# Down products of three SwiGLU half-steps as seven products of quarters

## The chip, the cores and the metric

One core of one Trainium2 chip runs the whole program. The metric is device time in microseconds (us) of one execution; the kernel before was timed three times. TensorE is called PE here, VectorE DVE, ScalarE ACT, GpSimd POOL and SyncE, which issues the loads, SP.

## The reference

A trunk of two layers over 512 tokens of width 1024, in float32. Each layer is three steps, each ending in a LayerNorm: a SwiGLU half-step, token mixing, and another SwiGLU half-step. There are four half-steps in all, with weights of their own; `D_FF` is 2816.

```python
def swiglu(x, w_gate, w_up, w_down):
    return (jax.nn.silu(x @ w_gate) * (x @ w_up)) @ w_down
...
    for l in range(DEPTH):
        x = layer_norm(DEEPNORM_ALPHA * x + 0.5 * swiglu(x, ffn_w_gate[l, 0], ffn_w_up[l, 0],
                                                         ffn_w_down[l, 0]),
                       ln_g[l, 0], ln_b[l, 0])
...
        x = layer_norm(DEEPNORM_ALPHA * x + mix, ln_g[l, 1], ln_b[l, 1])
        x = layer_norm(DEEPNORM_ALPHA * x + 0.5 * swiglu(x, ffn_w_gate[l, 1], ffn_w_up[l, 1],
                                                         ffn_w_down[l, 1]),
                       ln_g[l, 2], ln_b[l, 2])
```

## The kernel before

Every float32 product is made of three passes in a rounded format (`mm3`, line 120): each operand is split into a high part and the rest, and high x high, high x rest and rest x high are summed in one PSUM bank. The split of an operand (`split`, line 88) takes one ACT instruction for the high part (line 90) and one DVE instruction for the rest (line 92). Weights come by 512 KB loads on SP's queue (`fetch`, line 102) into four buffers `raw`, and are split (`halves`, line 107) into five pairs of buffers `whi` and `wlo`. A load can go out as soon as its buffer is free, ahead of its use.

The four half-steps are calls of `ffn` (line 214): the first ends near 385 us of the profiled span, the mixing of layer 0 fills 385 to 610 us, half-steps 2 and 3 end near 985 and 1350, the mixing of layer 1 near 1475, and half-step 4 ends the program. A half-step has two parts:

- Up products: 11 groups `fg` of 256 columns of the gate and the up weights. A group takes four loads and 96 `mm3` passes' matmuls of 512 tokens into four of the eight PSUM banks. Then ACT makes a tanh (line 251) and DVE the gated product `th` (lines 252 and 254), which is split into `act[f]` (128 rows of h transposed, 512 tokens). All 22 chunks of `act` are kept.
- Down products: all eight banks hold the result, four token tiles by two halves of 512 columns. For each of the 22 chunks `F` one load of 128 full rows of the down weights serves 4 x 2 x 3 matmuls (`down`, line 260). The last four chunks are kept loaded and the token tiles are finished one after another; after each, `ln_tile` (line 151) adds the two banks to `alpha*x` on DVE (line 158), lets ACT sum squares (line 164), DVE scale (lines 167 and 176) and POOL work out the factor (lines 168, 140 and 141). The transposes of the new x back into `xh` and `xl` (`to_xt`, line 126) wait in a list, and `flush` puts them between later products; the last two tiles' transposes fall into the next part's first products, which start with the first 256 tokens for that reason. `load_next` (line 113) asks for the next part's first weights.

The order of the work on an engine comes from a scheduler, which places an instruction when what it waits for is ready and takes the one written earlier where several are. Only inside `as_written` (line 73) is the order of an engine that of the program; half-step 1 uses that for PE, the others do not. POOL issues no DMAs. In half-step 1 the parameters of the state-space mixer are prepared beside the products (`s5_prepare`, called at group 1), with DMAs of their own. Layer 0's mixing spills x to DRAM, and half-step 2 loads it back (`x_back`, line 1150) in the place where the program has it, between up and down products.

## Time and profile before

| | us |
|---|---|
| median of three runs | 1847.7 (1847.27 to 1848.16) |
| the profiled execution, its span | 1845.7 |
| PE busy | 1818.3 |
| DVE busy | 898.4 |
| ACT busy | 637.0 |
| POOL busy | 32.2 |

The span runs from the first to the last instruction of one execution. Matmuls are pipelined, so PE counts as busy while any matmul is in it. L12 in a row is line 12 of the kernel; `<-` stands between what an instruction writes and what it reads, and, in brackets or after the idle time, ahead of what ended a wait. A line can be that of a helper: all splits have lines 90 and 92.

### The profile page before, as it was taken

The page shows a single profiled execution, that of the slowest core. Times are in us where ns is not written, and L with a number is a line of the kernel's source. Part 1 is how long each engine was busy: PE and PEld are TensorE (multiplying, and loading weights), DVE is VectorE, ACT ScalarE, POOL GpSimd, SP SyncE. Part 2 cuts the span into 40 slices and gives each one's busy share as a digit, 9 for nine tenths or more (in the row PEclk, how much of TensorE's full clock was granted, in tenths as well). Part 3 has the DMA queues.
Part 4 walks back from the last instruction along what each step waited for, and adds up shares of the span by engine and source line. Part 5 has one row for each costly group of instructions (what it writes and reads, how often), then busy time and mean ns, then how long its engine had stood idle before and what let it go on. Part 6 is the DMA issues. An engine that isn't in the chain of part 4 may idle for free.

```text
span 1845.7 us, 22332 instructions
## 1 busy us (share of the span) xinstructions
PE 1818.3 (99%) x8896; PEld 1523.2 (83%) x8896; DVE 898.4 (49%) x1531; ACT 637.0 (35%) x971; POOL 32.2 (2%) x119
## 2 busy tenths in 40 slices
PE   8999999999999999999999999999999999999998
PEld 7888888888877888888889888888878898888886
DVE  7856542267766644433227334432388554343324
ACT  3233421246675432222115223221264332222211
POOL 0000000000000000000000000000010000000000
PEclk9999999999999999999999999999999999999999
DMA  6345623264412633332323333323333153333231
GB/s 206 105 125 166 205 96 103 91 193 132 153 55 92 205 115 100 95 102 93 98 97 104 102 94 100 97 98 93 118 101 104 47 149 92 103 92 103 92 103 57
DMA packets 158968, 206.48 MB, mean 112 GB/s; under 512 B 7696, under 2 KB 129808, under 8 KB 158864
## 3 DMA queue, kind: packets, MB, share of 16 engines
q1 hardware_dynamic: 158864, 205.06, 36.3%
q8 instruction: 69, 1.13, 0.3%
q14 instruction: 35, 0.29, 0.0%
HBM read 189.83 MB, written 14.16 MB: 111 GB/s over the span
## 4 chain that ended last, share of the span: by engine, by line
PE 72%; issue 22%; DVE 3%; ACT 1%; DMA 1%; POOL 1%; POOLq 0%; SPq 0%; DVEq 0%; ACTq 0%
PE ps L122 23%; PE ps L123 23%; PE ps L124 23%; PE ps L131 1%; PE ps L650 1%; DVE wlo L92 1%; DMA s5tl<-side 1%; PE ps L698 0%; POOL rs L141 0%; PE ps L690 0%; DMA x<-in_x_dram 0%; DVE pl L92 0%; ACT ps L164 0%; PE ps L689 0%; ACT whi L90 0%
## 5 line engine op out<-in xcount | busy, mean ns | idle before, releaser
L92 DVE TENSOR_TENSOR wlo<-raw,whi 128x1024 fp32r<-128x1024 f32 x313 | 382.6, 1222 | 593.0 <-ACT whi L90 592.0
L122 PE MATMUL ps<-xh,whi 128*128 128x512 f32 (+1 forms) x1696 | 635.9, 376 | 0.7 <-ACT xh L90 0.7
L123 PE MATMUL ps<-xl,whi 128*128 128x512 f32 (+1 forms) x1696 | 633.4, 374 | 2.8 <-DVE xl L92 2.8
L124 PE MATMUL ps<-xh,wlo 128*128 128x512 f32 (+1 forms) x1696 | 633.2, 374 | 0.0
L90 ACT ACTIVATE whi<-raw 128x1024 fp32r<-128x1024 f32 x313 | 330.7, 1058 | 823.0 <-PE ps L123 470.3
L122 PEld LDWEIGHTS ps<-xh,whi 128*128 128x128 f32 x1696 | 319.2, 189 | 59.8 <-issue 3.1
L123 PEld LDWEIGHTS ps<-xl,whi 128*128 128x128 f32 x1696 | 320.3, 189 | 58.0 <-DVE xl L92 3.3
L124 PEld LDWEIGHTS ps<-xh,wlo 128*128 128x128 f32 x1696 | 320.2, 189 | 56.7
L122 PE MATMUL ps<-whi,act 128*128 128x512 f32 x656 | 255.5, 390 | 0.0
L124 PE MATMUL ps<-whi,act 128*128 128x512 f32 x656 | 255.2, 389 | 0.0
L123 PE MATMUL ps<-wlo,act 128*128 128x512 f32 x656 | 255.2, 389 | 0.0
L124 PEld LDWEIGHTS ps<-whi,act 128*128 128x128 f32 x656 | 123.2, 188 | 25.5
L123 PEld LDWEIGHTS ps<-wlo,act 128*128 128x128 f32 x656 | 123.2, 188 | 25.4
L122 PEld LDWEIGHTS ps<-whi,act 128*128 128x128 f32 x656 | 123.2, 188 | 25.4
L252 DVE SCALAR_TENSOR_TENSOR th<-th,ps 128x512 f32<-128x512 f32 x88 | 59.8, 683 | 113.4 <-ACT th L251 113.4
L251 ACT ACTIVATE th<-ps 128x512 f32<-128x512 f32 x88 | 51.9, 595 | 155.1 <-PE ps L124 155.1
L254 DVE TENSOR_TENSOR th<-th,ps 128x512 f32<-128x512 f32 x88 | 59.7, 686 | 92.8 <-PE ps L124 92.8
L92 DVE TENSOR_TENSOR act<-th,act 128x512 fp32r<-128x512 f32 x82 | 52.7, 684 | 0.0
L122 PE MATMUL ps<-whi,xh 128*128 128x256 f32 (+1 forms) x160 | 49.6, 312 | 2.0 <-ACT whi L90 1.5
L123 PE MATMUL ps<-wlo,xh 128*128 128x256 f32 (+1 forms) x160 | 49.1, 307 | 2.2 <-DVE wlo L92 2.2
L90 ACT ACTIVATE act<-th 128x512 fp32r<-128x512 f32 x82 | 47.2, 617 | 7.6 <-DVE th L254 7.5
L124 PE MATMUL ps<-whi,xl 128*128 128x256 f32 (+1 forms) x160 | 48.5, 304 | 0.0
(303 smaller groups left out, 1360.2 us busy)
## 6 DMA issues: line engine op xcount, KB each, us to landing
raw<-in_wg_dram SPq DMA_DIRECT2D x88, 512.0 KB, 3.8
raw<-in_wu_dram SPq DMA_DIRECT2D x88, 512.0 KB, 3.8
raw<-in_wd_dram SPq DMA_DIRECT2D x88, 512.0 KB, 3.2
raw<-in_ab_in_dram SPq DMA_DIRECT2D x20, 512.0 KB, 4.5
raw<-in_cd_in_dram SPq DMA_DIRECT2D x12, 512.0 KB, 3.7
x<-in_x_dram SPq DMA_DIRECT2D x8, 512.0 KB, 6.7
s<-zf SPq DMA_DIRECT2D x8, 512.0 KB, 5.2
raw<-in_ab_out_dram SPq DMA_DIRECT2D x8, 512.0 KB, 4.2
```

The costliest lines, as they stand in the source:

```text
L90: nc.scalar.activation(out=hi, in_=src, func=AF.Copy, scale=scale)
L92: nc.vector.tensor_tensor(out=lo, in0=src, in1=hi.bitcast(F32), op=ALU.subtract)
L122: mm(ps, ah, bh, start=start, stop=False)
L123: mm(ps, ah, bl, start=False, stop=False)
L124: mm(ps, al, bh, start=False, stop=stop)
L131: self.nc.tensor.transpose(p[:, j * P:(j + 1) * P], src[:, k * P:(k + 1) * P], self.ident)
L251: nc.scalar.activation(out=th, in_=bk[0, f], func=AF.Tanh, scale=0.5)
L252: nc.vector.scalar_tensor_tensor(out=th, in0=th, scalar=1.0, in1=bk[0, f], op0=ALU.add, op1=ALU.mult)
L254: nc.vector.tensor_tensor(out=th, in0=th, in1=bk[1, f], op=ALU.mult)
L650: nc.tensor.matmul(banks[h][:, o:o + w], a[r, i * P:i * P + P], b[r, :w], start=n == 0, stop=n == 2)
```

## The change

Half-steps 2 to 4 call a new function `ffn7`. It sees the down product as a product of matrices of 2 x 2 blocks: h in two halves of 256 tokens and in even and odd chunks, the down weights in even and odd chunks (b1, b2) and two halves of 512 columns. Seven products of quarters take the place of eight. Of the seven weights three are quarters of the given ones and four are sums of quarters, `T1` to `T4`, kept in DRAM: `down_sums` copies quarters there and adds others onto them with DMAs that add, all issued from POOL. It is a generator in four steps, taken at every third group of up products one half-step ahead (`ahead`). The seven sums of h are made by DVE in `hb` after each group (four operations of 256 columns more than before) and split at once into a slot `sl` of 7 x 256 columns.

The 11 pairs of chunks are taken in three groups of 3, 4 and 4. A group's seven products run after the up product that follows the group's last (the last group's right after the last up product), so up and down products alternate. Each product is made for two token tiles of 128 in two banks; three of the seven (`P6`, `N3`, `P7`) go on top of what a bank holds already, after DVE has added it to x. `ln_tile` is cut into its addition (`add_to`) and the rest (`ln_rest`). `take` adds a finished pair of banks to the right quarter of x, with the sign. In the last group the LayerNorms of the first two token tiles are placed ahead of the last two products, and those of the other two behind each half of the last. PE's order is that of the program in `ffn7`. Half-step 1 and the mixers are unchanged. Comments and docstrings are removed.

```diff
-    def mm3(self, ps, ah, al, bh, bl, start, stop):
-        mm = self.nc.tensor.matmul
+    def mm3(self, ps, ah, al, bh, bl, start, stop, onto=False):
+        mm = partial(self.nc.tensor.matmul, skip_group_check=onto)
...
+    def add_to(self, zz, p, scale, total=None):
+        self.nc.vector.scalar_tensor_tensor(out=zz, in0=p, scalar=scale, in1=zz, op0=ALU.mult, op1=ALU.add,
+                                            **({} if total is None else {"accum_out": total}))
...
+                    if fg % 3 == 1:
+                        next(ahead, None)
...
+    def down_sums(self, wd):
+        dma = self.nc.gpsimd.dma_start
+        wv = wd.rearrange("(j two p) d -> two p j d", two=2, p=P)
+        b11, b12, b21, b22 = (wv[i][:, :, c:c + 512] for i in range(2) for c in (0, 512))
+        T = [self.dram.tile([P, NF // 2, 512], F32, name=f"T{i}_{len(self.sums)}") for i in range(1, 5)]
+        self.sums.append(T)
+        t1, t2, t3, t4 = T
+        for t, src in ((t3, b22), (t1, b12), (t2, b11), (t4, b21)):
+            dma(t, src)
+        yield
+        dma(t3, b12, accum_op=ALU.add)
+        dma(t1, b11, accum_op=ALU.add)
+        yield
+        dma(t2, t3, accum_op=ALU.add, max_dma_last_dim=2048)
+        yield
+        dma(t4, t2, accum_op=ALU.add, max_dma_last_dim=2048)
+    def ffn7(self, xt, wg, wu, wd, g_ap, b_ap, T, out=None, fetch=None, ahead=iter(()), groups=(3, 4, 4)):
+        nc, tc = self.nc, self.tc
+        tt = nc.vector.tensor_tensor
+        wv = wd.rearrange("(j two p) d -> two p j d", two=2, p=P)
+        t1, t2, t3, t4 = T
+        prod = {"P1": (0, wv[0][:, :, 0:512]), "P2": (1, wv[1][:, :, 0:512]), "Q5": (3, t1), "P6": (4, t2),
+                "N3": (6, wv[1][:, :, 512:]), "P7": (5, t3), "Q4": (2, t4)}
+        first = [sum(groups[:i]) for i in range(len(groups) + 1)]
+        with tc.tile_pool(name="act", bufs=1, reuse_waits="tile") as ap, \
+                tc.tile_pool(name="at", bufs=2, reuse_waits="tile") as at:
+            slots = {}
+            def up(fg):
+                bk, jobs = {}, []
+                for m, W in enumerate((wg, wu)):
+                    Wv = W.rearrange("(k p) f -> p k f", p=P)
+                    for f in range(2):
+                        bk[m, f] = self.bank()
+                    wt = [self.load(Wv[:, kh * 4:kh * 4 + 4, fg * 256:fg * 256 + 256], [4, 256]) for kh in range(2)]
+                    jobs.append(([(bk[m, f], f) for f in range(2)],
+                                 lambda k, f, wt=wt: [w[:, k % 4, f * P:f * P + P] for w in wt[k // 4]]))
+                    if not self.pending:
+                        self.cols(*jobs.pop())
+                if jobs:
+                    for m in range(2):
+                        self.cols(*jobs[m], 0, 256)
+                        self.flush(1 - m)
+                    for m in range(2):
+                        self.cols(*jobs[m], 256, SEQ)
+                hb = at.tile([P, 8, 256], F32, name="hb")
+                for f in range(2):
+                    th = at.tile([P, SEQ], F32, name="th")
+                    nc.scalar.activation(out=th, in_=bk[0, f], func=AF.Tanh, scale=0.5)
+                    nc.vector.scalar_tensor_tensor(out=th, in0=th, scalar=1.0, in1=bk[0, f],
+                                                   op0=ALU.add, op1=ALU.mult)
+                    tt(out=hb[:, 0::7] if f == 0 else hb[:, 1:3], in0=th.rearrange("p (a c) -> p a c", a=2),
+                       in1=bk[1, f].rearrange("p (a c) -> p a c", a=2), op=ALU.mult)
+                tt(out=hb[:, 3], in0=hb[:, 7], in1=hb[:, 2], op=ALU.subtract)
+                tt(out=hb[:, 5], in0=hb[:, 0], in1=hb[:, 7], op=ALU.subtract)
+                tt(out=hb[:, 4], in0=hb[:, 3], in1=hb[:, 0], op=ALU.subtract)
+                tt(out=hb[:, 6], in0=hb[:, 1], in1=hb[:, 4], op=ALU.add)
+                sl = ap.tile([P, 2, 7, 256], F32R, tag="sl", name="sl", bufs=max(groups) + 1)
+                self.split(hb[:, 0:7], sl[:, 0], sl[:, 1])
+                slots[fg] = sl
+            def fetch_w(name, js):
+                src = prod[name][1][:, js[0]:js[-1] + 1]
+                return self.load(src, [len(js), 512])
+            def part(name, banks, js, start, stop, w=None, ts=(0, 1)):
+                hi, lo = w or fetch_w(name, js)
+                b = prod[name][0]
+                for i, j in enumerate(js):
+                    for t in ts:
+                        c = slice(t * P, t * P + P)
+                        self.mm3(banks[t], slots[j][:, 0, b, c], slots[j][:, 1, b, c], hi[:, i], lo[:, i],
+                                 start and i == 0, stop and i == len(js) - 1, name in ("P6", "P7", "N3"))
+            def down(gi, ln):
+                last = gi == len(groups) - 1
+                js = list(range(first[gi], first[gi + 1]))
+                units = [js[i:i + 2] for i in range(0, len(js), 2)]
+                two = lambda: [self.bank() for _ in range(2)]
+                s = [self.sm.tile([P, 6], F32, name="st") for _ in range(NT)] if last else None
+                def take(banks, half, col, scale, total=None):
+                    for t in range(2):
+                        i = 2 * half + t
+                        self.add_to(xt[i][:, col * 512:col * 512 + 512], banks[t], scale,
+                                    s[i][:, total:total + 1] if last and total is not None else None)
+                def whole(name, banks, start=True):
+                    for u in units:
+                        part(name, banks, u, start and u is units[0], u is units[-1])
+                X, Y = two(), two()
+                if last:
+                    V = two()
+                    names = (("P1", X), ("P2", Y), ("Q5", V))
+                    for u in units:
+                        for name, bk in names:
+                            part(name, bk, u, u is units[0], u is units[-1])
+                    take(X, 0, 0, 0.25)
+                    take(Y, 0, 0, 0.25, 0)
+                else:
+                    whole("P1", X)
+                    take(X, 0, 0, 0.25)
+                    whole("P2", Y)
+                    take(Y, 0, 0, 0.25)
+                    V = two()
+                    whole("Q5", V)
+                take(V, 1, 1, 0.25)
+                whole("P6", X, False)
+                take(X, 0, 1, -0.25)
+                whole("N3", V, False)
+                take(V, 0, 1, 0.25, 1)
+                if last:
+                    g, b = self.ln_params(g_ap, b_ap)
+                def norm(t, junk):
+                    self.ln_rest(t, xt[t], s[t], junk, g, b, None if out is None else out[t * P:(t + 1) * P])
+                if last:
+                    norm(0, [V[0]] * 2)
+                    norm(1, [V[1]] * 2)
+                whole("P7", X, False)
+                take(X, 1, 1, -0.25, 1)
+                take(X, 1, 0, 0.25)
+                Z = two()
+                if not last:
+                    whole("Q4", Z)
+                    take(Z, 1, 0, 0.25)
+                    return
+                ws = [fetch_w("Q4", u) for u in units]
+                for t in range(2):
+                    for u, w in zip(units, ws):
+                        part("Q4", Z, u, u is units[0], u is units[-1], w, (t,))
+                    self.flush(1)
+                    self.load_next()
+                    self.add_to(xt[2 + t][:, 0:512], Z[t], 0.25, s[2 + t][:, 0:1])
+                    norm(2 + t, [Z[t]] * 2)
+            with self.as_written(mybir.EngineType.PE):
+                gi = 0
+                for fg in range(NF // 2):
+                    up(fg)
+                    if fg == 0 and fetch is not None:
+                        xt = fetch()
+                    if fg % 3 == 0:
+                        next(ahead, None)
+                    if gi < len(groups) - 1 and fg == first[gi + 1]:
+                        down(gi, False)
+                        gi += 1
+                down(gi, True)
...
-        k.ffn(None, wg[0, 0], wu[0, 0], wd[0, 0], ln_g[0, 0], ln_b[0, 0], spill=s0, side=side, fetch=x_again)
+        k.ffn(None, wg[0, 0], wu[0, 0], wd[0, 0], ln_g[0, 0], ln_b[0, 0], spill=s0, side=side, fetch=x_again,
+              ahead=k.down_sums(wd[0, 1]))
...
-        k.ffn(xt, wg[0, 1], wu[0, 1], wd[0, 1], ln_g[0, 2], ln_b[0, 2], fetch=x_back)
+        k.ffn7(xt, wg[0, 1], wu[0, 1], wd[0, 1], ln_g[0, 2], ln_b[0, 2], k.sums[0], fetch=x_back,
+               ahead=k.down_sums(wd[1, 0]))
         first(cd_in, 1024, 512)
-        k.ffn(xt, wg[1, 0], wu[1, 0], wd[1, 0], ln_g[1, 0], ln_b[1, 0])
+        k.ffn7(xt, wg[1, 0], wu[1, 0], wd[1, 0], ln_g[1, 0], ln_b[1, 0], k.sums[1],
+               ahead=k.down_sums(wd[1, 1]))
         first(wg[1, 1], 0, 256)
         k.mix_cd(cd_in, cd_out, pool_w, pool_s, sgu_ln, wsT, b_s, xt, ln_g[1, 1], ln_b[1, 1])
-        k.ffn(xt, wg[1, 1], wu[1, 1], wd[1, 1], ln_g[1, 2], ln_b[1, 2], out=out)
+        k.ffn7(xt, wg[1, 1], wu[1, 1], wd[1, 1], ln_g[1, 2], ln_b[1, 2], k.sums[2], out=out)
```

## Rows read from the trace of the kernel before

**Rows 1.** The page: busy time by engine, TensorE's clock in 40 slices.

```profile
PE 1818.3 (99%) x8896; PEld 1523.2 (83%) x8896; DVE 898.4 (49%) x1531; ACT 637.0 (35%) x971; POOL 32.2 (2%) x119
...
PEclk9999999999999999999999999999999999999999
```

**Rows 2.** What PE waited for, longest first: us in total, times, longest.

```profile
PE ps L131 <- DMA x<-in_x_dram: 6.1, 2, 4.4
```

**Rows 3.** Windows: up, then down products of half-step 2; busy us by engine.

```profile
core 0: us, PE busy (x) PEld busy (x) DVE busy (x) ACT busy (x) POOL busy (x), PEclk, DMA share, GB/s
700.00:760.00 60.00, 60.00 (x267) 49.69 (x266) 25.04 (x29) 17.72 (x23) 0.00 (x0) 1.00 0.34 99
900.00:950.00 50.00, 50.00 (x223) 41.40 (x222) 11.03 (x9) 9.55 (x9) 0.00 (x0) 1.00 0.29 100
```

**Rows 4.** Timeline of PE, down products: start, us, instruction; twelve apart.

```profile
880.12 0.39 PE L122 MATMUL ps<-whi,act 128*128 128x512 f32 x1
...
882.84 0.39 PE L122 MATMUL ps<-whi,act 128*128 128x512 f32 x1
```

**Rows 5.** Chain that ended last, half-step 2's end: start, us, what.

```profile
981.82 0.87 PE ps L131 x8
...
985.21 0.23 PE ps L124
985.67 0.12 PE ps L124
...
991.18 0.87 PE ps L131 x8
```

**Rows 6.** What the load queue (SP) waited for: us in total, times, longest.

```profile
SPq L104 <- DVE wlo L92: 1243.0, 267, 22.3
```

**Rows 7.** By line and shape, 620 to 980 us (last: whole): busy, mean ns.

```profile
L92 DVE TENSOR_TENSOR wlo<-raw,whi 128x1024 fp32r<-128x1024 f32 x65 | 79.7, 1226 | 150.3 <-ACT whi L90 150.1
L254 DVE TENSOR_TENSOR th<-th,ps 128x512 f32<-128x512 f32 x22 | 15.0, 687 | 27.0 <-PE ps L124 27.0
L92 DVE TENSOR_TENSOR act<-th,act 128x512 fp32r<-128x512 f32 x22 | 14.1, 684 | 0.0
L158 DVE SCALAR_TENSOR_TENSOR xb<-ps,xb 128x512 f32<-128x512 f32 x6 | 4.1, 692 | 3.8 <-PE ps L124 3.7
...
L90 ACT ACTIVATE whi<-raw 128x1024 fp32r<-128x1024 f32 x65 | 68.9, 1060 | 199.6 <-PE ps L123 116.6 <-PE ps L124 78.0 <-issue 2.8
L90 ACT ACTIVATE act<-th 128x512 fp32r<-128x512 f32 x22 | 12.5, 615 | 0.0
...
L485 DVE TENSOR_TENSOR xs<-xs 128x256 f32<-128x256 f32 x1 | 0.4, 426 | 0.0
```

**Rows 8.** Timeline of DVE: LayerNorm of tile 0 at half-step 2's end.

```profile
967.37 0.69 DVE L158 SCALAR_TENSOR_TENSOR xb<-ps,xb 128x512 f32<-128x512 f32 x1 [2.02 <-PE ps L124]
...
971.15 1.28 DVE L176 SCALAR_TENSOR_TENSOR zf<-zf,rs,lnb 128x1024 f32<-128x1024 f32 x1 [0.37 <-POOL rs L141]
```

**Rows 9.** Timeline of DVE: LayerNorm of the last tile.

```profile
1837.47 0.69 DVE L158 SCALAR_TENSOR_TENSOR xb<-ps,xb 128x512 f32<-128x512 f32 x1 [0.24 <-PE ps L124]
...
1841.25 1.41 DVE L173 SCALAR_TENSOR_TENSOR zf<-zf,rs,lnb 128x512 f32<-128x512 f32 x2 [1.51 <-POOL rs L141]
```

**Rows 10.** Timeline of POOL; loads of x back: count, ns, first and last issue.

```profile
0.99 0.46 POOL L491 MEMSET side<- 16x448 f32 x1
...
369.27 0.19 POOL L168 TENSOR_TENSOR st<-st 128x1 f32<-128x1 f32 x1 [358.68 <-ACT ps L164]
...
L1150 SPq DMA_DIRECT2D xb<-s x4: 320/362/478, 619.9 to 641.9; - x4
```

**Rows 11.** Windows: half-step 1.

```profile
0.00:369.00 369.00, 360.58 (x1700) 301.59 (x1701) 200.77 (x497) 113.28 (x143) 1.51 (x13) 1.00 0.44 137
```

**Rows 12.** Chain that ended last: first transposes ending half-steps 2 and 3.

```profile
975.49 0.88 PE ps L131 x8
...
1339.86 0.87 PE ps L131 x8
```

14 lines of the change are left out of this document (8 added, 6 removed).

## The prediction

> **What bounds the kernel now.** I read the page's totals first. TensorE (PE) is busy for 1818.3 of 1845.7 us and its clock was granted at the full level in every slice; VectorE (DVE) is busy for half the span and ScalarE (ACT) for a third [rows 1]. Next the waits: of all that PE waited for, the largest entry is 6.1 us in two waits for the first tiles of x [rows 2]. So no other engine holds PE back now, and a matmul that is taken away shortens the span by its whole spacing, unless the change makes a new wait. The stages confirm it: in 60 us of up products and in 50 us of down products of half-step 2, PE is busy throughout, DVE for 25.0 and 11.0 us, and the DMA engines for 0.34 and 0.29 of the time at about 100 GB/s [rows 3]. The reader should keep two things from there: PE has no gap to fill, and DVE has room on average, which says nothing of short stretches.
>
> **Matmuls removed.** The spacing of the down products is the distance of two starts, 882.84 - 880.12 = 2.72 us for 12 matmuls, 0.2267 us each [rows 4]. A half-step's down products are now 22 chunks x 4 token tiles x 2 halves x 3 passes = 528 matmuls. The change makes seven products of 11 chunks x 2 token tiles x 3 passes = 462, of the same shape (128 stationary columns, 512 moving). That is 66 x 0.2267 = 15.0 us for each of three half-steps: **-44.9 us**. Up products, transposes and LayerNorm counts stay. The order of PE is now pinned to the program's; around the end of half-step 2 it already went as the program has it (down products, transposes of the second tile at 981.82, last matmul at 985.21, then narrow up products from 985.67, the third tile's transposes at 991.18) [rows 5], so I cost the pin at nothing; where the scheduler's freedom had hidden a late operand, the price is that operand's lateness, 0 to 3 us for a half-step, which I count in the DVE terms below.
>
> **Weights in the down products.** Seven quarters instead of four are loaded and split: 7 x 11 = 77 half-width chunks against 44. A load of two chunks (512 KB) now serves 12 matmuls, 2.72 us, where one of the same size served 24. Supply: 0.524 MB / 2.72 us = 193 GB/s. Down loads (4 KB pieces) ran at 100 GB/s with 0.29 of the engines, 345 GB/s if they were full; up loads (1 KB pieces) at 99/0.34 = 291 [rows 3]. The 2 KB pieces lie between, so the down products need 0.56 to 0.66 of the engines while they run. At present the loads wait for a free buffer, not for the bus: the load queue spent 1243 us in 267 waits on DVE's releases [rows 6]. With nothing else on the bus I cost this at nothing; with something else, see the second rival.
>
> **DVE in a group of down products.** Prices [rows 7]: split of two chunks 1.226 us, of one 0.684; adding a bank to x 0.692; each multiplication of h 0.687; a 128x256 operation between SBUF tiles 0.426. The new split of seven quarters (1792 columns) has no row; along the line through 512 and 1024 columns, 1.06 ns a column, it is 2.04 us. For the group of three chunks: 7 x (1.226 + 0.684) = 13.4 us of splits, 16 additions of 0.69 = 11.0, the h work left after the up product (2 x 0.687 + 4 x 0.426 + 2.04) = 5.1, the first two splits for the next up product 2.5; less 3.1 for the splits made ahead (five buffers, two in use) and 1.4 for two additions that may come after: 27.5 us. PE takes 7 x 18 x 0.2267 = 28.6. That is 96% of DVE; a late split makes PE wait. Bounds 0 and 5 us, I take 1. The groups of four have 30.7 (17.2 + 11.0 + 5.1 + 2.5 - 3.7 - 1.4) against 38.1 us and are covered. The h work of the last up product is not one product ahead as in the other groups: 3.1 us on DVE, the ACT split (1.7 us on the line through its 512 and 1024 columns [rows 7]), 2.04 on DVE, about 7 us in all; ahead of its first use stand 42 matmuls, 9.5 us. Covered by 2.5 us, no cost. Additions to x stand one product (4.1 or 5.4 us) ahead of the next use of their bank and take 1.4 to 2.8 us: no cost either.
>
> **The end of a half-step.** The last group also has the LayerNorms. From the last matmul of product N3 to the transposes of tile 0 stand P7 (24) and a first half of Q4 (12 matmuls), 8.2 us. The chain of a tile took from the addition at 967.37 to the end of its last operation at 971.15 + 1.28, 5.1 us [rows 8]. So 3.1 us are spare, and DVE has about 12 us of work in the stretch (two LayerNorms, six additions, two splits), not all of it due there. Bounds 0 and 4 us a half-step, I take 2. Tiles 2 and 3 now follow each other at 2.7 us, not 5.4; in the next half-step's first up product they are due later than that, so no cost. At the kernel's end it counts: the last addition starts at 1837.47 and the final operations at 1841.25 [rows 9]; tile 2's last 1.41 us may now lie in tile 3's way. Bounds -0.7 (one addition less behind tile 3) and 1.4, I take 1.
>
> **The sums in DRAM.** Each set is four copies and four additions, each of 128 x 11 x 512 x 4 B = 2.88 MB, issued from POOL; three sets are 24 transfers. They have no PE, DVE or ACT work. The trace shows no DRAM-to-DRAM transfer and none from POOL. One transfer of that size takes the 16 engines 8.4 us at the rate of the down loads, 9.9 us at that of the up loads [rows 3]; an addition reads its target as well, so 8.4 to 19.8. Sum 202 to 356 us of all engines. Where they run matters: the code puts steps at every third group of up products, but what waits for nothing is moved forward. The loads of x back from DRAM, written behind all eleven up products of half-step 2, were issued at 619.9 to 641.9, and POOL's fill of line 491, which belongs to the second group, at 0.99 us [rows 10]. So I expect the twelve copies of all three sets near the kernel's start. There they share the bus with the first loads of x, for which PE waited twice [rows 2]: half the bus doubles a few us. Bounds 0 and 8, I take 3.
>
> **Sum.** -44.9 + 3 x 1 + 3 x 2 + 1 + 3 = -31.9 on the profiled span of 1845.7 us: 1813.8. The median of the runs is 2.0 us above the span, so **1816**. With all terms at their ends the case reaches from 1802 to 1839; 1802 to 1826 is its own range.
>
> **Rival 1, slower: POOL's queue.** POOL works out the factor of each LayerNorm in three small steps, the first of them at 369.27 [rows 10]. If all 24 transfers stand ahead of it, with each addition waiting in POOL's queue for what it adds to, then the LayerNorm of half-step 1 waits for nearly all of the 202 to 356 us, and PE with it, for the transposes and mixer need x. Until 369 us the kernel's own loads leave 56% of the engines, 207 us [rows 11]. Nothing is lost if the transfers need less. At 320 us, 93 us are lost (320 - 207, less some 20 for the last, which need only be issued): about 1910. It is slower than before from about 259 us on, 10.8 us a transfer (207 + 20 + the 32 us gained); at 356 us 1945, more if DRAM to DRAM is slower than any load shown. For it: the early issue of what waits for nothing [rows 10]; even the sums for half-step 4 wait for nothing but their own copies. Against it: sets 2 and 3 may be placed behind the LayerNorm, and at the rate of the down loads all is over in time.
> The Trainium skill, DMA: Bandwidth & Descriptors, "Anatomy of one DMA — SWDGE (gpsimd) path", says that DMA engines never wait on a semaphore: the wait is held by the issuing sequencer before it dispatches. This speaks against the change; by that rule the additions' waits stand in front of POOL's arithmetic and the time would be this rival's 1910, where transfers that hold up nothing leave it at 1816. The load queue's waits agree with it [rows 6]; no run here shows it for POOL.
>
> **Rival 2, DVE or the bus binds in the down products.** If splits come late in all nine groups, or transfers of a set run during down products, PE waits there. Price: 3 us in each of nine groups, less the 9 us that the sum has, is 18; or, where loads get half the bus (146 to 173 GB/s against 193), 0.6 us for each of 14 loads, 8 us for a group of four, less what lies ready. Either way some 20 us: **1836**. For it: 96% in the group of three. Against it: the room in the groups of four.
> The same page, "Queues, rings and completion order", says that an engine serves its queues in turn, a packet at a time. By that rule loads would keep about half of a shared bus, which is the second price; up products, at 99 GB/s, would lose nothing. No run here shows two queues of data at once.
>
> **Rival 3, the gain is eaten.** The products are fewer, but the copies slow the first half-step (where 44% of the bus is used [rows 11]) and half-step 2 waits for its sums by about as much as is saved: 1848.
>
> **Chances.** Forecast 0.50 (1802 to 1826), rival 2 0.13 (1826 to 1844), rival 3 0.06, rival 1 0.31, about half of it above 1900. The range 1802 to 1900 leaves out some 0.15 above and 0.03 below. A measurement of this kernel can tell 0.2%, 3.7 us, from no change: faster 0.63, same 0.06, slower 0.31.
>
> **What would show it.** Right: 462 down matmuls at 0.227 us in half-steps 2 to 4, each of them some 349 to 353 us long instead of 364 (the first tile's transposes at the ends of half-steps 2 and 3 stand at 975.49 and 1339.86 [rows 12]), PE's waits under 5 us a half-step, POOL's first LayerNorm step soon after ACT's squares. Wrong: POOL waiting on a DMA near 369 us, PE idle behind it for tens of us; or PE waiting for weight splits inside the groups; or the DMA share at its top in the first half-step with PE below 99%.

## The result, and the profile after

The changed kernel took 1990.2 us (median; 1989.6 to 1990.9) against 1847.8 us before: a ratio of 1.077, 95% interval 1.076 to 1.079, so **142 us slower**. Forecast were 1816 us and a range of 1802 to 1900. The profiled execution has a span of 1987.7 us.

The page: busy time, the forty slices of TensorE (PE), its clock and the DMA engines, and the two queues that carry data.

```profile
PE 1801.5 (91%) x8698; PEld 1503.3 (76%) x8698; DVE 1094.1 (55%) x1810; ACT 712.0 (36%) x998; POOL 68.7 (3%) x143
...
PE   5965436699999999999999999999999999999997
...
PEclk8977768899999999999999999999999999999998
DMA  9999999733264324525353442535344333343533
...
q1 hardware_dynamic: 173264, 231.02, 38.2%
q0 software_dynamic: 25728, 69.21, 14.2%
```

Before, the clock row was full from end to end [rows 1]. Now the first eight slices hold the whole loss, and in the first seven of them the DMA engines are full. After them PE is as busy as it was. q0 holds the 24 transfers of the sums: 14.2% of 1987.7 us is 282 us of all 16 engines.

A stage is measured here from one fourth LayerNorm factor on POOL to the next, the last one to the end of the span. "HS" is a SwiGLU half-step, "ab" and "cd" are the two mixers; the runs below the second are the experiments. The time is the median of a kernel's runs, the stages are those of its profiled run; e2, e4, e5 and e8 were run once.

```
run                   time    HS1    ab     HS2    HS3    cd     HS4
before              1847.8   392.3  233.9  364.5  364.7  124.5  365.9
after               1990.2   562.4  233.2  357.2  358.9  118.6  357.4
e1_no_sums          1817.9   391.3  233.7  357.6  357.2  118.6  357.0
e2_sums_alone       2014.9   559.5  234.0  364.5  364.4  124.5  366.5
e3_paced            1831.7   393.4  242.5  358.4  356.5  118.6  358.6
e4_small_packets    1960.4   534.1  233.1  357.7  358.0  118.6  357.2
e5_burst            1874.1   439.6  233.0  364.0  359.2  118.6  357.6
e6_paced_up         1823.6   392.4  235.7  358.6  358.5  118.6  357.9
e7_onto             1834.8   393.4  234.3  362.5  362.8  121.9  356.0
e8_warm_burst       1878.8   450.0  235.3  357.9  357.7  118.6  357.5
e9_next_early       1822.9   392.0  233.8  359.8  355.6  119.3  357.8
e11_where_written   1871.8   426.7  233.9  366.1  365.5  118.6  358.6
e12_no_takes        1822.8   392.4  233.4  357.4  358.1  121.5  357.1
e13_groups          1852.6   393.2  233.9  369.2  369.3  123.4  362.5
```

Half-step 1, whose own code did not change, lost 170.1 us. HS2 to HS4 with the mixer between them gained 1219.5 - 1192.1 = 27.4 us. (The marker stands later at the end of a half-step of seven products, since token tiles 2 and 3 finish last and together; cd, which begins at such a marker and ends at an old one, gets that back as 5.9 us.)

Windows of half-step 1 after (columns as in [rows 3]; before, the first 369 us had PE busy for 360.58 at full clock, with a DMA share of 0.44 [rows 11]):

```profile
0.00:46.00 46.00, 24.79 (x128) 22.17 (x128) 7.67 (x8) 8.71 (x10) 9.47 (x19) 0.83 0.97 354
46.00:92.00 46.00, 41.30 (x219) 36.23 (x220) 37.62 (x173) 11.45 (x17) 2.62 (x2) 0.91 1.10 237
...
230.00:276.00 46.00, 0.00 (x0) 0.00 (x0) 5.30 (x9) 4.70 (x6) 2.22 (x2) 0.50 1.06 312
...
369.00:539.00 170.00, 170.00 (x752) 140.77 (x751) 53.97 (x61) 44.68 (x52) 0.00 (x0) 1.00 0.37 119
```

While the DMA share is near 1.0 or above, PE stands for a part of each window, in one altogether, and there its clock is granted at 0.50, the lower of its two levels; in the others the mean is 0.76 to 0.91. Once the share is down at 0.37, PE is full again. Over the first 369 us PE is busy for 214.75 and stands for 154, against 8 before; the other 24 of the 170 us lost are, by the difference, work done at the lower clock.

The timeline of POOL (start, us, instruction, and in brackets what it waited for): set 1 begins at 1.45, set 2 at 71.81 and 109.29, set 3 at 184.99 and 220.16; the last transfer is issued at 336.44, long before half-step 1's first LayerNorm.

```profile
1.45 1.24 POOL L303 DMA_DIRECT2D T<-in_wd_dram  x1 [0.38 <-issue]
2.88 3.35 POOL L303 DMA_DIRECT2D T<-in_wd_dram  x3
...
70.95 1.50 POOL L308 DMA_DIRECT2D T<-T  x1 [39.06 <-DMA T<-in_wd_dram]
...
109.29 3.86 POOL L303 DMA_DIRECT2D T<-in_wd_dram  x3
...
336.44 1.50 POOL L310 DMA_DIRECT2D T<-T  x1 [37.91 <-DMA T<-T]
539.03 0.19 POOL L178 TENSOR_TENSOR st<-st 128x1 f32<-128x1 f32 x1 [201.09 <-ACT ps L174]
```

So all 24 transfers, additions too, ran in the first 370 us, although half of them are written in half-steps 2 and 3. POOL held each addition until what it reads had landed (39.06 us), which agrees with the rule of the Trainium skill named under rival 1 (DMA: Bandwidth & Descriptors, "Anatomy of one DMA — SWDGE (gpsimd) path"); but it was through by 338 us and then waited 201 us for ScalarE (ACT). So POOL's queue was not what the LayerNorm waited for.

What PE waited for until 560 us: in total, times, longest.

```profile
PE ps L716 <- DVE xs L712: 88.5, 3, 58.4
PE ps L127 <- DVE wlo L94: 41.1, 7, 11.5
PE ps L125 <- ACT whi L92: 9.5, 3, 7.2
```

88.5 us are three waits at L716, the matmul that makes a quarter of the S5 matrices (the parameters of the state-space mixer that half-step 1 prepares). The next two rows and 1.7 us at L126, 52.3 us together, are late weights. The chain that ended last shows what stands behind the first kind (start, us, what): a row of small round trips through DRAM, one after the other.

```profile
244.79 8.70 DMA side<-side
...
257.09 22.14 DMA s5tl<-side
...
280.05 9.95 DMA s5cl<-side
```

DMA issues until 369 us (count, KB each, median us from issue to landing), before and then after: the round trips took four times as long, the loads of the up weights 5.6 times.

```profile
raw<-in_wu_dram SPq DMA_DIRECT2D x22, 512.0 KB, 4.0
...
side<-side SPq DMA_DIRECT2D x32, 32.0 KB, 2.0
...
s5tl<-side SPq DMA_DIRECT2D x4, 256.0 KB, 4.8
```

```profile
raw<-in_wu_dram SPq DMA_DIRECT2D x20, 512.0 KB, 22.4
...
side<-side SPq DMA_DIRECT2D x29, 32.0 KB, 7.6
...
s5tl<-side SPq DMA_DIRECT2D x3, 256.0 KB, 20.1
```

The round trips go out on SP's queue, between the weight loads (start of the issue, us, instruction):

```profile
256.49 0.38 SPq L106 DMA_DIRECT2D raw<-in_wu_dram  x1
257.09 0.34 SPq L699 DMA_DIRECT2D s5tl<-side  x1
```

The 512 KB load landed after 20.2 us, at 276.7, and the 256 KB round trip behind it at 279.2, while SP's queue moved 1.90 MB in the 23 us from 257 to 280, 83 GB/s. So much of the 22.14 us may be the weight loads ahead in its own queue, which had become slow; no run gives the round trips a queue of their own.

And the two queues in the window from 46 to 92 us (packets, MB, share of 16 engines):

```profile
q0 software_dynamic: 3474, 7.42, 82.5%
q1 hardware_dynamic: 3470, 3.45, 27.6%
```

As many packets of the one as of the other. A packet of a transfer held its engine for 0.825 x 46 x 16 / 3474 = 0.175 us, one of a load for 0.0585 us (the shares add up to 1.10, so packets overlap a little). The loads, in 1 KB packets, got 3.45 MB in 46 us, 75 GB/s, where the same window had 104 GB/s before. The rule of the Trainium skill (DMA: Bandwidth & Descriptors, "Queues, rings and completion order") that an engine serves its queues in turn, a packet at a time, agrees with these counts; they show equal shares by number, not how many of the profile's packets make up a turn. What a share is worth hangs on the length of its packets, and the transfer's packet is three times as long as that of a load.

### The profile page after: what moved, and what is told of

Its sections match the earlier page's. It is cut to its first block, busy times and chain, and to the rows that moved or that the text cites. A ratio compares the mean times of both kernels' runs of the same rounds, so it can differ in the third digit from the quotient of the medians.

```text
span 1987.7 us, 22527 instructions
## 1 busy us (share of the span) xinstructions
PE 1801.5 (91%) x8698; PEld 1503.3 (76%) x8698; DVE 1094.1 (55%) x1810; ACT 712.0 (36%) x998; POOL 68.7 (3%) x143
## 3 DMA queue, kind: packets, MB, share of 16 engines
q0 software_dynamic: 25728, 69.21, 14.2%
## 4 chain that ended last, share of the span: by engine, by line
issue 54%; PE 22%; DMA 15%; DVE 6%; ACT 2%; POOL 1%; SPq 0%; DVEq 0%; POOLq 0%; ACTq 0%
DMA raw<-in_wg_dram 7%; PE ps L125 7%; PE ps L126 7%; PE ps L127 7%; DMA s5tl<-side 3%; DMA s5r<-side 2%; DVE wlo L94 1%; DMA s5r<-xs 1%; DMA side<-side 1%; PE ps L820 1%; POOL rs L144 1%; DMA s5cl<-side 1%; PE ps L868 0%; ACT whi L92 0%; ACT ps L174 0%
## 5 line engine op out<-in xcount | busy, mean ns | idle before, releaser
L94 DVE TENSOR_TENSOR wlo<-raw,whi 128x1024 fp32r<-128x1024 f32 (+1 forms) x373 | 443.2, 1191 | 420.2 <-ACT whi L92 419.4
L92 ACT ACTIVATE whi<-raw 128x1024 fp32r<-128x1024 f32 (+1 forms) x373 | 385.5, 1035 | 750.2 <-PE ps L126 263.6
L126 PE MATMUL ps<-xl,whi 128*128 128x512 f32 (+1 forms) x1696 | 642.1, 379 | 7.6 <-DVE xl L94 7.4
L126 PEld LDWEIGHTS ps<-xl,whi 128*128 128x128 f32 x1696 | 326.6, 193 | 64.5 <-DVE xl L94 9.2
L125 PE MATMUL ps<-whi,sl 128*128 128x512 f32 x462 | 179.9, 389 | 0.0
L126 PE MATMUL ps<-wlo,sl 128*128 128x512 f32 x462 | 179.8, 389 | 0.0
L127 PE MATMUL ps<-whi,sl 128*128 128x512 f32 x462 | 179.7, 389 | 0.0
L163 DVE SCALAR_TENSOR_TENSOR xb<-ps,xb 128x512 f32<-128x512 f32 x152 | 97.6, 683 | 8.5 <-PE ps L127 8.5
L127 PEld LDWEIGHTS ps<-whi,sl 128*128 128x128 f32 x462 | 86.7, 188 | 18.2
L126 PEld LDWEIGHTS ps<-wlo,sl 128*128 128x128 f32 x462 | 86.7, 188 | 17.9
L125 PEld LDWEIGHTS ps<-whi,sl 128*128 128x128 f32 x462 | 86.7, 188 | 17.8
L350 DVE SCALAR_TENSOR_TENSOR th<-th,ps 128x512 f32<-128x512 f32 x66 | 44.9, 684 | 86.2 <-ACT th L349 86.2
L94 DVE TENSOR_TENSOR sl<-hb,sl 128x1792 fp32r<-128x1792 f32 x33 | 66.8, 2024 | 43.5 <-ACT sl L92 43.5
L352 DVE TENSOR_TENSOR hb<-th,ps 128x512 f32<-128x512 f32 x66 | 44.9, 688 | 82.4 <-PE ps L127 82.4
L716 PE MATMUL ps<-xs 128*16 128x128 f32 x32 | 6.7, 382 | 88.5 <-DVE xs L712 88.5
L92 ACT ACTIVATE sl<-hb 128x1792 fp32r<-128x1792 f32 x33 | 56.1, 1700 | 59.3 <-DVE hb L357 59.3
L716 PEld LDWEIGHTS ps<-xs 128*16 128x16 f32 x32 | 3.8, 128 | 91.4 <-DVE xs L712 89.8
```

Source lines behind the costliest of these rows:

```text
L92: nc.scalar.activation(out=hi, in_=src, func=AF.Copy, scale=scale)
L94: nc.vector.tensor_tensor(out=lo, in0=src, in1=hi.bitcast(F32), op=ALU.subtract)
L125: mm(ps, ah, bh, start=start, stop=False)
L126: mm(ps, ah, bl, start=False, stop=False)
L127: mm(ps, al, bh, start=False, stop=stop)
L163: self.nc.vector.scalar_tensor_tensor(out=zz, in0=p, scalar=scale, in1=zz, op0=ALU.mult, op1=ALU.add, **({} if total is None else {"accum_ ...
```

## The experiments

**Theory A**: what costs time is where the transfers run; brought forward to the first 370 us they starve half-step 1. Its rivals: the order of instructions in half-step 1 (B), a fixed price for each transfer wherever it runs (C), POOL's queue (rival 1 of the prediction).

**e1_no_sums.** The sums left out.

```diff
-        t1, t2, t3, t4 = T
+        t1, t2, t3, t4 = wv[0][:, :, 512:], wv[0][:, :, 0:512], wv[1][:, :, 512:], wv[1][:, :, 0:512]
...
-              ahead=k.down_sums(wd[0, 1]))
```

> The seven products take plain quarters of the down weights where the changed kernel takes the sums T, and the 24 transfers are left out (the down products of half-steps 2 to 4 are then not the reference's; their instructions, loads and bytes are the same). Theory A (the transfers, all issued in the first 340 us, starve half-step 1's weight loads and the S5 round trips on the 16 DMA engines): the first LayerNorm factor on POOL goes back from 539 to 369 us, half-steps 2 to 4 keep their gains of 7.3, 5.8 and 8.5 us, and the time is 1847.8 - 21.6 = 1826 us (1820 to 1830). Rival B (what costs time is the order that the planner gives to half-step 1's own instructions, or the products themselves, and the transfers are hidden): near 1990 us.

1817.9 us, 0.984 of before (0.983 to 0.986), half-step 1 as before. It is 8 us under the expectation, which had left out what cd gives back. Everything but the sums comes to 1817.9 where the forecast, less its 3 us for the sums, says 1813: the sums cost 172 us.

**e2_sums_alone.** The other half: the 24 transfers, and the down products of before.

```diff
-        k.ffn7(xt, wg[0, 1], wu[0, 1], wd[0, 1], ln_g[0, 2], ln_b[0, 2], k.sums[0], fetch=x_back,
+        k.ffn(xt, wg[0, 1], wu[0, 1], wd[0, 1], ln_g[0, 2], ln_b[0, 2], fetch=x_back,
                ahead=k.down_sums(wd[1, 0]))
```

> The 24 transfers at the places of the changed kernel, and the down products of half-steps 2 to 4 as they were before (the sums are made and not used). Theory A: half-step 1 loses its 170 us by the transfers alone, so 1847.8 + 170 = 2018 us (2008 to 2028), with the first LayerNorm factor at about 539 us. Rival B: 1848 us, since the seven products are not there.

2014.9 us (one run): 167 us more than before, all of it in half-step 1. With e1's 172 us the two halves add up, and B is out; SP's queue also issues half-step 1's DMAs in the same order in the changed kernel as in e1.

**e3_paced.** Each transfer waits for an ACT instruction: six of set 1 among half-step 1's down products, its last two (`T<-T`, one sum added onto another) in the attention stage of the mixer ab, those of sets 2 and 3 one to a group of up products in half-steps 2 and 3.

```diff
+    def behind(self, steps):
+        ins = self.nc.cur_bb.bb.instructions
+        act = next(i for i in reversed(ins) if i.engine == mybir.EngineType.Activation)
+        last = ins[-1]
+        next(steps, None)
+        start = next(k for k in reversed(range(len(ins))) if ins[k] is last) + 1
+        info = mybir.DependencyInfo(mybir.DependencyClass.Sync, mybir.DependencyReason.DATA)
+        for i in ins[start:]:
+            if i.engine == mybir.EngineType.Pool:
+                self.tc.add_manual_dep(i, act.name, info, reason="behind")
...
+                if F in (0, 2, 4, 6, 8, 12):
+                    self.behind(ahead)
...
+            ahead[1, 3] = ahead[4, 3] = (self.behind, sums)
...
+                    if 0 < fg < 9:
+                        self.behind(ahead)
```

> The same transfers and products, but every transfer waits for a ScalarE instruction near the place where it is written: the six of set 1 that read the weights among the down products of half-step 1 (from about 255 us), the two T<-T ones in the attention stage, sets 2 and 3 one transfer to a pair of hidden tiles in half-steps 2 and 3. Theory A, with the refinement that loads of 4 KB packets (down products of half-step 1) keep enough of the engines, and that one transfer of 10 to 20 us at a time is covered by the four raw weight buffers (4 x 5.3 us): 1826 to 1834 us, first LayerNorm factor at 369 to 374 us. Rival C (each transfer costs the weight loads the same wherever it is put, 170 us for 282 us of engine time): about 1990 us. Rival 1 of the prediction (a transfer that waits in POOL's queue holds a LayerNorm behind it): stalls of ACT or DVE on POOL at the ends of half-steps, 1850 us and more.

1831.7 us, 0.991 of before (0.990 to 0.993): the same bytes at other times, and 158 us are gone. C is out, and so is rival 1, whose price here was 1850 us and more. Of the 13.8 us that are left over e1, 8.9 stand in the attention stage, and PE's waits there name it:

```profile
PE ps L125 <- DMA sth<-s5ch: 5.9, 1, 5.9
```

**e4_small_packets.** The transfers in packets of half the length, to see how the engines share.

```diff
+        def dma(t, src, **kw):
+            for c in (0, 256):
+                self.nc.gpsimd.dma_start(t[:, :, c:c + 256], src[:, :, c:c + 256], **kw)
```

> The changed kernel with each transfer cut into two halves of 256 columns, so that its packets are half as long; places, bytes and sums as they are. Theory A with packets taken in turn by the engines (one of the transfer, one of a load): an accumulating packet that took 0.173 us for 2 KB takes about 0.09 us for 1 KB, a load then gets 1 KB of every 0.146 us on each engine, 112 GB/s and more than the 104 that half-step 1 used before, so most of the 170 us comes back and what is left is the S5 round trips: 1850 to 1910 us. If a packet costs the same 0.17 us at half the length: loads get the same 75 GB/s for twice as long, up to 2150 us. If the engines share by bytes and not by packets: 1990 us.

1960.4 us (one run): only 30 us came back, not most of it. The two queues from 46 to 92 us:

```profile
q0 software_dynamic: 5517, 7.11, 81.1%
q1 hardware_dynamic: 4267, 4.24, 33.7%
```

A shorter packet did hold its engine for less (0.108 us) and the loads got 92 GB/s in place of 75, so they share by packets and not by bytes. The counts are equal only in part of the window (1418 each from 80 to 92 us); in the rest the transfers are ahead. But the last transfer was then issued at 416 us in place of 336, and PE still waited 74.2 us at the S5 matmul. The expectation took the S5 round trips for a remainder. They are the larger part.

**e5_burst.** One set in each of three places.

```diff
+                    if fg == burst:
+                        for _ in range(8):
+                            self.behind(ahead)
```

> One set of eight transfers back to back in each of three places: set 1 at the start of half-step 1 as in the changed kernel (weight loads and S5 round trips beside it), set 2 from the first up products of half-step 2 and set 3 from the fifth of half-step 3 (weight loads alone beside them). Theory A, that the loss is the weight loads at 75 GB/s of the 99 to 104 they need: 120 us of burst are short by 2.9 to 3.5 MB, of which four raw buffers hold 2 MB, so 9 to 15 us a set in half-steps 2 and 3, more where a down group needs 193 GB/s (up to 25 us), and 25 to 57 us for set 1, where the S5 round trips wait as well: 1818 + 43 to 110 = 1860 to 1930 us. Rival C (a set costs a third of 170 us wherever it runs): 1990 us. Rival D (only the S5 round trips lose time, weight loads are covered): half-steps 2 and 3 at 357 us each as without the sums, 1843 to 1875 us in all.

1874.1 us (one run): set 1 at the kernel's start cost 48 us, set 2 in half-step 2 cost 6.4, and half-step 3 with set 3 is 2.0 longer (table, against e1). Beside the bursts in half-steps 2 and 3, and in half-step 1 until 417 us:

```profile
740.00:760.00 20.00, 20.00 (x89) 16.54 (x89) 8.04 (x11) 6.08 (x7) 0.00 (x0) 1.00 1.09 257
...
1200.00:1250.00 50.00, 50.00 (x223) 41.39 (x222) 29.05 (x35) 17.48 (x18) 3.20 (x2) 1.00 1.07 307
```

```profile
PE ps L127 <- DVE wlo L94: 18.0, 5, 8.3
PE ps L125 <- ACT whi L92: 8.5, 3, 7.1
```

With the engines full (1.09, 1.07) PE did not stand: the weight buffers were full when the burst began, for in the 38 us before set 3 the load queue had waited 26.2 us for DVE to release one. From 1178 to 1340 us, a whole group of down products among it, PE has no wait at all, so the 2.0 us are not set 3's (without any transfer there, half-step 3 is 358.9 in after); beside set 2 it waited 4.1 us for weights. At the kernel's start the buffers are empty, and PE waits for weights, without a wait at the S5 matmul. The time lies in the ranges of A and of D, but neither has it right: the 9 to 15 us a set that A gave half-steps 2 and 3 did not come, and D has no loss without an S5 wait.

**e6_paced_up.** The two T<-T transfers of set 1 moved out of the attention stage, the last of sets 2 and 3 into the next half-step (the edit is shown against e3).

```diff
-            ahead[1, 3] = ahead[4, 3] = (self.behind, sums)
...
-                    if 0 < fg < 9:
-                        self.behind(ahead)
+                    if fg < 9:
+                        self.behind(late if fg < 2 else ahead)
```

> The paced kernel with the two T<-T transfers of a set moved: for set 1 out of the attention stage into the first two up products of half-step 2, for sets 2 and 3 the last one into the next half-step. The paced kernel lost 8.9 us in the attention stage, where its trace has a 5.9 us wait of TensorE for a 256 KB S5 load; theory A says that this loss goes and no other comes: 1831.7 - 9 = 1823 us (1819 to 1826). If the two transfers cost the same beside the up products: 1832 us.

1823.6 us, 0.987 of before (0.985 to 0.988): as expected, 24 us faster than the kernel before, with the sums at 6 us over e1.

**e8_warm_burst.** Set 1 in one burst where the weight buffers are full and the S5 round trips run; the rest paced.

```diff
+                    if fg == 4:
+                        for _ in range(8):
+                            self.behind(ahead)
```

> The paced kernel of 1823.6 us with set 1's first transfers moved: all eight back to back behind the fourth pair of hidden tiles of half-step 1 (from about 95 us, 120 us long), where the raw weight buffers are full and the S5 round trips run; sets 2 and 3 stay paced. A burst with full buffers and no S5 beside it cost 6.3 us in half-step 2 and 2.0 us in half-step 3; set 1 at the kernel's start, with the buffers empty, cost 47 us and its trace shows no wait of TensorE for S5. Theory S (in the changed kernel sets 2 and 3 lose most by the S5 round trips: 88.5 us of TensorE's waits there are for the S5 matrices): half a share for one set, 25 to 50 us, 1848 to 1873 us, with TensorE waiting for xs at the S5 matmul. Theory W (only weight loads count, full buffers cover them): 2 to 8 us, 1825 to 1832 us.

1878.8 us (one run), half-step 1 longer by 57.5 than in e6. PE's waits until 440 us:

```profile
PE ps L729 <- DVE xs L725: 48.8, 3, 32.5
PE ps L134 <- DMA x<-in_x_dram: 6.3, 2, 4.2
PE ps L126 <- DVE xl L94: 2.1, 1, 2.1
```

No late weights at all, and 48.8 us at the S5 matmul. Theory S holds in its place and kind; the price was above its 25 to 50 us, and W's 2 to 8 us are out.

**e11_where_written.** The changed kernel with its steps held where its program has them.

```diff
-                        next(ahead, None)
+                        self.behind(ahead)
```

> The changed kernel with each of its four steps of a set held behind the ScalarE instruction before the place where its program writes the step (pairs 1, 4, 7 and 10 in half-step 1; 0, 3, 6 and 9 in half-steps 2 and 3), so that the planner can't bring it forward; nothing else. Theory A: half-steps 2 and 3 lose 0 to 3 us each as with one step at a time; half-step 1 has its four copies in the first pairs and adds beside the S5 round trips, 10 to 25 us: 1818 + 10 to 30 = 1828 to 1848 us. If the place of the transfers doesn't matter: 1990 us. If their place matters only through the S5 round trips: 1843 us and more.

1871.8 us, 1.013 of before (1.012 to 1.015), above the 1828 to 1848 expected. The four copies at 42 us cost nothing (PE 45.86 of 46 us busy), now that the buffers had been filled first; one wait of 29.6 us at the S5 matmul makes up most of the 34 us of half-step 1. HS2 and HS3 lost 8 us each, more than expected: two additions were issued together while a down group ran, and half-step 2 has 5.4 us of waits for weights and banks during and just behind that group. So 118 of the 172 us come from the transfers being moved forward; 54 are in the places as written.

**Theory E**: at the end of a half-step VectorE (DVE) works through takes, LayerNorm and splits in one queue and sets the time. In the changed kernel PE stood as follows at the end of half-step 2, and then, in windows of 2 us, ran at half clock from 1144 to 1150 with 11 or 12 matmuls in a window and not 20:

```profile
1141.75 0.39 PE L125 MATMUL ps<-xh,whi 128*128 128x256 f32 x1 [0.74 <-ACT xh L92]
1144.57 0.58 PE L126 MATMUL ps<-xl,whi 128*128 128x256 f32 x1 [2.44 <-DVE xl L94]
```

```profile
1146.00:1148.00 2.00, 2.00 (x12) 2.00 (x11) 1.42 (x2) 0.55 (x1) 0.74 (x2) 0.50 0.48 168
1148.00:1150.00 2.00, 2.00 (x11) 2.00 (x11) 2.00 (x6) 1.46 (x2) 0.00 (x0) 0.50 0.00 0
...
1152.00:1154.00 2.00, 2.00 (x20) 2.00 (x19) 0.38 (x1) 0.55 (x2) 1.17 (x3) 1.00 0.93 308
```

**e7_onto.** Q4 summed onto P7's banks, 12 us less for DVE. (This edit and the three after it are shown against e6.)

```diff
+                ws = [fetch_w("P7", u) for u in units]
+                for t in range(2):
+                    by_tile("P7", t, ws)
+                    self.add_to(xt[2 + t][:, 512:], X[t], -0.25, s[2 + t][:, 1:2] if last else None)
                 ws = [fetch_w("Q4", u) for u in units]
                 for t in range(2):
+                    by_tile("Q4", t, ws)
```

> The kernel of the run above with Q4 summed onto P7's banks, both by token tile: per group two takes of 0.683 us less on VectorE, 12.3 us of VectorE in the kernel, and in the last group of a half-step 1.37 us less of the work that stands in front of the split of tile 1's xl, for which the first up product waits 2.44 us. Theory E (VectorE's queue at a half-step's end sets its length; the seven products fell 5 us short of the forecast there): 1.4 to 3 us less for each half-step, 4 to 9 us less than the run above, about 1817 us. If the loss at the end is the LayerNorm's own latency: the same time as the run above within 2 us; if TensorE now waits for P7's takes before Q4: up to 1 us more for each of nine groups.

1834.8 us, 11 us slower than e6. DVE is 9 us less busy, and PE waits for the take that frees the bank, which in e6 cost it 1.2 us; this is the last case of the expectation, at somewhat more than its price, and says nothing of theory E:

```profile
PE ps L125 <- DVE xb L163: 15.4, 12, 2.6
```

**e9_next_early.** The next stage's weight chunks split ahead of Q4.

```diff
+                for _ in range(2):
+                    self.load_next()
                 for t in range(2):
...
-                    self.load_next()
```

> The paced kernel of 1823.6 us with the next stage's two weight chunks split ahead of Q4's products in the last group instead of one behind each token tile: the second chunk's wlo split, 1.22 us of VectorE, leaves the place in front of tile 1's xl, for which the first up product waits 2.44 us. Theory E (VectorE's order at the end of a half-step): about 1.2 us less at the ends of half-steps 2 and 3, with the wait down to 1.2 us, 1819 to 1823 us. If the splits now stand in front of the LayerNorm of tile 0 or 1 instead: the transposes wait for zf by as much, no change.

1822.9 us (0.986 of before, 0.985 to 0.988): no difference to e6 that can be measured, though the time also lies in theory E's range. The wait for xl that was to fall to 1.2 us is 2.02.

**e12_no_takes.** Two takes left out.

```diff
-                take(X, 1, 0, 0.25)
+                if not last:
+                    take(X, 1, 0, 0.25)
```

> The paced kernel of 1823.6 us without the two takes of P7 into the first column half of token tiles 2 and 3 in the last group of a half-step (that part of the sum is left out, so the result is not the reference's). They are 1.28 us of VectorE in front of tile 0's and tile 1's xl; the first up product waits 0.74 us for xh and 2.44 us for xl, and TensorE then runs at its half clock for some 3 us. Theory E (VectorE's queue sets the end of a half-step): the waits fall to about 2 us, 1.3 us less a half-step and up to 2.5 us where the clock stays up, 1816 to 1820 us. Rival (the LayerNorm's latency through ScalarE and GpSimd sets it): 1822 to 1825 us.

1822.8 us; HS2 to HS4 with cd come to 1194.1 against 1193.6 in e6. PE at half-step 2's end:

```profile
975.45 0.39 PE L125 MATMUL ps<-xh,whi 128*128 128x256 f32 x1 [2.90 <-ACT xh L92]
976.47 0.39 PE L126 MATMUL ps<-xl,whi 128*128 128x256 f32 x1 [0.63 <-DVE xl L94]
```

The wait moved from DVE's xl to ACT's xh and stayed 3.5 us long (3.2 before), and the time is that of the rival. But the order on ACT changed as well. In e6 the four splits of xh stand together; here a square of token tile 2's LayerNorm, which itself waits for DVE, came ahead of the third, for which PE waits (ACT's timeline in this run):

```profile
971.72 1.06 ACT L92 ACTIVATE xh<-ps 128x512 fp32r<-128x512 f32 x2
974.10 0.69 ACT L174 ACTIVATE ps<-xb,st 128x512 f32<-128x512 f32 x1 [1.32 <-DVE st L171]
974.82 0.58 ACT L92 ACTIVATE xh<-ps 128x512 fp32r<-128x512 f32 x1
```

So the run shows that leaving out these two takes gains nothing under this scheduler; it neither shows nor refutes theory E.

**e13_groups.** A longer last group, as cover.

```diff
-    def ffn7(... groups=(3, 4, 4), late=iter(())):
+    def ffn7(... groups=(3, 3, 5), late=iter(())):
...
-                sl = ap.tile(... bufs=max(groups) + 1)
+                sl = ap.tile(... bufs=5)
```

> The paced kernel of 1823.6 us with groups of 3, 3 and 5 pairs of hidden tiles in place of 3, 4 and 4 (five slots as before). P7 and Q4 of the last group, which run while the LayerNorm of tiles 0 and 1 is made, are 60 products and not 48, 13.6 us in place of 10.9, and VectorE's work beside them is the same. Theory E and its rival alike: 2.7 us more cover takes the 3.2 us of waits in front of the first up product to under 1 us, and the stretch at half clock with it, 3 to 5 us a half-step at the ends of half-steps 2 and 3, up to 2 at the kernel's end; the second group of 3, in which VectorE is 96% busy, costs 1 us a half-step: 1813 to 1819 us. If a group of 3 costs more than that because VectorE is the bound there: 1823 us and more.

1852.6 us, 1.003 of before (1.002 to 1.004) and 29 us slower than e6. The forecast missed, and the other case has the side but not the cause: until 960 us, with both groups of 3 behind it, PE has only 4 us of waits in half-step 2. The largest wait stands in front of the second matmul of Q4, for the first of its weights. ACT had its half of that split done at 970.2 us; DVE came to it at 975.42, behind the LayerNorm of tiles 0 and 1 and the additions of P7:

```profile
975.42 2.35 DVE L94 TENSOR_TENSOR wlo<-raw,whi 128x1024 fp32r<-128x1024 f32 x2
...
976.70 0.79 PE L126 MATMUL ps<-wlo,sl 128*128 128x512 f32 x1 [5.39 <-DVE wlo L94]
```

Here the order on DVE does set the time. That Q4 of five pairs keeps three weight chunks at once out of five buffers may be why its split comes so late; no run separates this.

What makes the ends of half-steps 2 and 3 late by 3 us and more stays open: no run takes work off DVE there and leaves the order of the other engines as it was.

## Why the prediction was wrong

**Matmuls removed: right.** 462 down matmuls a half-step, and PE full in the groups at the forecast spacing. The pin of PE's order was not tested by itself; its price would be among PE's waits of half-steps 2 to 4, which are short but for those at the ends.

**Weights and DVE in the down products: right.** In after, half-steps 2 to 4 show waits for late weight splits of 3.0 us in all, where 1 us each was taken. The new split of 1792 columns took 2.02 us for the forecast 2.04.

**The end of a half-step: mechanism right, size too small.** e1 stands for the whole sum without transfers: 1219.5 - 1190.5 = 29.0 us gained in half-steps 2 to 4 and cd, against 44.9 - 3 - 6 - 1 = 34.9. The missing 5.9 us are here. 2 us a half-step were taken, but at the end of half-step 2 the waits of 3.2 us are followed by a stretch at half clock (6 us in after, which is 3 us of work again; some 3.4 us in e1, by the same working 1.7); half-step 3 has 3.5 us of short waits at full clock, 2.2 of them late splits. The working let PE stand and then go on at full speed. At the kernel's own end 2 + 1 us were taken and 5.5 are lost: from the start of the last matmul to the end of the span it is 8.7 us before and 14.2 in e1. DVE comes to the last tile's addition 0.4 us after that matmul before [rows 9] and 3.4 after it in e1, behind the additions of P7 and the first part of tile 2's LayerNorm. With 0.8 us of other late splits that makes 14.7 (3.2 + 1.7 + 3.5 + 5.5 + 0.8) of the 15.9 us by which e1 falls short of 44.9. The last matmul before, then the last matmul and that addition in e1:

```profile
1837.04 0.39 PE L124 MATMUL ps<-whi,act 128*128 128x512 f32 x1
...
1801.20 0.39 PE L127 MATMUL ps<-whi,sl 128*128 128x512 f32 x1
...
1804.62 0.68 DVE L163 SCALAR_TENSOR_TENSOR xb<-ps,xb 128x512 f32<-128x512 f32 x1
```

**The sums in DRAM: the step that failed.** Its size was right (282 us of 16 engines; bounds 202 and 356), and the early issue was seen. The cost was put at 3 us, with bounds of 0 to 8, and was 172. Three things were wrong with it. First, only the twelve copies were expected early. The additions wait for nothing but their copies, as rival 1 said two paragraphs on, so the sum used a milder case than the rival. Bringing the transfers forward is worth 118 of the 172 us (e11). Second, the cost was worked out from the loads of x alone. The weight loads of a kernel that starts with empty buffers were left out (48 us for one set there, in e5), and so were the S5 round trips, each of which waits for the one before it: 57 us for one set in e8, 88.5 us of waits in after. Third, a share of the bus was taken as a matter of bandwidth, in rival 1 as well: 207 us were called free because 56% of the engines were idle. For a chain of small transfers the time from issue to landing counts, 2.0 to 4.8 us each before and 7.6 to 20.1 after. What makes it up, the transfers' packets or the slowed weight loads ahead in the same queue, is not separated.

**Rival 1: the right side by the wrong mechanism.** Its condition, all transfers ahead of the LayerNorm, came true, and the 282 us are above its threshold of 259. But with 282 us its own sum gives 1816 + 282 - 207 - 20 = 1871, which is 119 short, and POOL was idle for 201 us before that LayerNorm. Its sentence that nothing is lost if the transfers fit into the idle engines is refuted by e8: 57 us lost in a place where they fit.

**Rival 2: right where it applies.** Up products at 99 GB/s lose nothing beside a burst, it said: 6.4 us in e5 with set 2 and nothing with set 3, where full buffers stood ahead. Its price in the down products did not show there either: set 3 ran beside a whole group of them without a wait. In e11 two additions issued together beside one cost its 8 us. Its half of the bus was 75 GB/s for loads of 1 KB, a quarter of the 291 that full engines would give them [rows 3]: a packet of the transfer holds its engine three times as long as one of the load.

**Rival 3** had the place, half-step 1, and a fifth of the price.

## What to carry to other kernels

Under a scheduler like this one a transfer that waits for nothing runs at the start of the program, not where it is written; if its time matters, tie it to an instruction of the stage where it should run, and look first for stages with full buffers and no chain of round trips. Here idle DMA engines were free only beside work that was loaded ahead: price a background transfer by the longest chain of small transfers beside it, each step at its time to landing under load, and not by the bytes. And when a run takes work off an engine, look whether the other engines kept their order before reading the time.

## What the runs showed of the hardware

- Two queues of data that both had work moved equal numbers of packets (3474 and 3470 in 46 us). A packet of DRAM-to-DRAM transfers, most of them accumulating, held its engine for 0.175 us, a 1 KB load for 0.0585 us.
- Beside such transfers, and on one queue with 512 KB loads that they slowed, a 32 KB DMA landed after 7.6 us in place of 2.0, one of 256 KB after 20.1 in place of 4.8.
- One set (23 MB of copies and additions) needed 94 us of 16 engines, 282 / 3, and could be run beside half-steps 2 and 3 with full weight buffers for 6.4 us (set 2 of e5) or without a wait of PE (set 3).
- A wait can cost more than its length: after two waits of 0.74 and 2.44 us PE's clock was granted at the lower level (0.50) for 6 us, in which it did about half the work.
